# Gated linear attention: scores times values for both 64-row chunks in one product, then the products with the states, alternating rows and columns of the array

## The chip, the cores and the metric

The kernel runs on one core of a Trainium2 chip as one program. The metric is device time in microseconds (us). A page of the profile describes one profiled execution; its span runs from the first to the last instruction of the program.

The engines are named as the profile names them: PE is the matmul engine (PEld its weight loads, which run beside the products), DVE the vector engine, ACT the scalar engine, POOL the general engine, SP the engine whose queue issues the loads from memory.

## The reference

A small network of two layers over 256 positions and 1024 channels, in fp32. Each layer is: half a gated feed-forward block (2816 wide), a mixer, half a second feed-forward block. The mixer of layer 0 has retention in one half of its width and gated linear attention (GLA) in the other; layer 1 has a gated recurrence and an mLSTM. The change touches GLA alone: four heads, key width 64, value width 128, chunks of 64 rows. For one head and chunk:

```
b = cumsum(log_a)                       # over the 64 rows
s = (q * exp(b - b_mid)) @ (k * exp(b_mid - b)).T ;  s = tril(s)
intra  = s @ v                          # 64 x 64 times 64 x 128
upd    = (k * exp(b_end - b)).T @ v     # 64 x 128
state' = exp(b_end) * state + upd       # from chunk to chunk
inter  = (q * exp(b)) @ state
out    = intra + inter
```

## The kernel before

The 256 positions are two tiles of 128 rows, t = 0 and t = 1, so each tile holds two GLA chunks (c = 0, 1). All large products (feed-forward, projections in and out of the mixers) are written by `mm3` (L192 to L200) and by `prod` (L513 to L522): weights and activations are split into a high part and a rest (L114, L115, on ACT and DVE), and a product is three matmuls over 512 columns, with all 128 rows and columns of the array. The even mixer projects in units of 512 columns or less (L993 to L1000). A unit's weights are loaded by SP into one of three raw buffers, split into one of five high/rest buffers, and used by tile 0 and, some 1.5 units later, by tile 1 (`LAG`, L30); a buffer is split into again once tile 1 has used it.

The small work of the mixers is written as generators (`gla_chain`, L766 to L873). They are advanced by `tick` (L159): every `mm3` counts its columns, and a step of a chain is put between the large products when its count has run down (`STEPS`, L46). So GLA's small products stand in PE's queue between the products of a projection. The framework lays out each engine's instruction order with a model of its own; `after(x)` (L385) asks that an instruction come behind x on its engine, without a semaphore.

The four heads are laid out in pairs: head hd = 2p + hh. Keys and queries of head hd lie in partitions hh·64 to hh·64+63 of block p, so a product that contracts over them uses the upper (hh = 0) or lower (hh = 1) 64 rows of PE's array. The output rows of chunk c are partitions c·64 to c·64+63 in PSUM, so a product that makes 64 of them uses the left (c = 0) or right (c = 1) 64 columns of the array. "Layout" below is the pair rows*columns that the profile gives for a product, as 64*64. Every fp32 product is two passes of weight load and matmul, and counts twice in the profile.

In `gla_chain`: the scores of both heads hh of a pair are made with 64 rows and 128 columns (L824) and copied through a mask into `gS{hh}` (L825), a 128 x 128 block for each p with chunk 0 and chunk 1 on its diagonal and zeros elsewhere. The states' updates are products of layout 64*64 (L837); the states `Sst[c]` are formed on DVE (L843, L846). In tile 0 there is no state for c = 0. Then, for each hh, p and c in turn, the output of 64 rows is made: scores times values, contracting over all 128 rows but with the 64 columns of the chunk (L866, layout 128*64), and at once, where there is a state, query times state (L869, layout 64*64). One PSUM tile for each hh takes the outputs and is copied to `og` (L870) before the next hh begins. `og` is normalised (L871, L872), gated (L969) and transposed (L988) later.

PSUM is two rings of four tiles, `ps` for the large products and `acc` for the small ones and for accumulations across units.

Of the kernel before, what the change touches and what calls it, by code (L numbers as in the profile page):

```python
# [19 lines left out]
P = 128  # L20
# [33 lines left out]
def f2(ap):  # L54
    return ap.rearrange("p a b -> p (a b)")
# [7 lines left out]
def hybrid_kernel(ctx: ExitStack, tc: tile.TileContext, I, out):  # L63
    nc = tc.nc
    V, S, T, G = nc.vector, nc.scalar, nc.tensor, nc.gpsimd
# [11 lines left out]
    def nm(s):  # L77
        cnt[0] += 1
        return f"{s}_{cnt[0]}"

    def ps_tile(shape=(P, 512), tag="ps"):
        return psum.tile(list(shape), F32, tag=tag, name=nm(tag))

    def mt(tag, shape, bufs=1, dt=F32):
        return pools[-1].tile(list(shape), dt, tag=tag, bufs=bufs, name=nm(tag))
# [293 lines left out]
    C = {}  # L379
# [5 lines left out]
    def after(ins):  # L385

        return tc.issue_after(ins.ins) if ins is not None else nullcontext()
# [322 lines left out]
    def logsigmoid(dst, z, pre, w, bufs=1):  # L710

        e = mt(pre + "e", [P, w], bufs)
        V.scalar_tensor_tensor(out=e, in0=z, scalar=-1.0, in1=z, op0=ALU.mult, op1=ALU.max)
        S.activation(e, e, AF.Exp, scale=-1.0)
        S.activation(e, e, AF.Ln, bias=one, scale=1.0)
        V.scalar_tensor_tensor(out=dst, in0=z, scalar=0.0, in1=e, op0=ALU.min, op1=ALU.subtract)

    def head_rms_scale(psO, name):

        sq = mt("sq", [P, 4, P], 1)  # L720
        S.activation(f2(sq), f2(psO), AF.Square)
        ss = mt("hss", [P, 4], 2)
        V.tensor_reduce(out=ss, in_=sq, axis=AX.X, op=ALU.add)
        return rsqrt_mean(ss, P, 4, name)

    def bc4(ap):
        return ap.unsqueeze(2).to_broadcast([P, 4, P])
# [8 lines left out]
    def even_units(w_in, w_lr_up, b_lr, w_out, nxt):  # L736
# [4 lines left out]
        def has(t, *keys):  # L741
            return lambda: all(k in st[t] for k in keys)
# [15 lines left out]
        def body_gq(t, ps, rs):  # L758
            gl = mt("gl", [P, 16])
            S.activation(gl, ps[:, 256:], AF.Copy, scale=rs)  # L760
            chain(gla_chain(t, gl))
            q = mt("gq", [P, 256])
            S.activation(q, ps[:, :256], AF.Copy, scale=rs)
            st[t]["q"] = q

        def gla_chain(t, gl):  # L766
            d = st[t]
            yield STEPS[0]
            pt = ps_tile(tag="acc")
            T.transpose(pt[:16, :P], gl, ident)  # L770
            glT = mt("glT", [16, P])
            V.tensor_copy(glT, pt[:16, :P])
            yield STEPS[1]
            pz = ps_tile(tag="acc")
            T.matmul(pz[:, :256], glT, C["lrup"], start=True, stop=True)
            la = mt("gz", [P, 256])
            V.tensor_tensor(out=la, in0=pz[:, :256], in1=C["blr"], op=ALU.add)
            logsigmoid(la, la, "g", 256)
            yield STEPS[2]

            pb = ps_tile(tag="acc")
            pe = ps_tile(tag="acc")
            T.matmul(pb[:, :256], C["cum"][:, 0:P], la, start=True, stop=True)
            T.matmul(pb[:, 256:], C["cum"][:, P:2 * P], la, start=True, stop=True)
            T.matmul(pe[:, :256], C["cum"][:, 2 * P:3 * P], la, start=True, stop=True)
            for p in range(2):
                T.matmul(pe[:, 256 + 2 * p:258 + 2 * p], la[:, p * P:(p + 1) * P], C["cum"][:, 3 * P:3 * P + 2],
                         start=True, stop=True)
            E1 = mt("E1", [P, 256])
            E2 = mt("E2", [P, 256])  # L790
            E3 = mt("E3", [P, 256], 2)
            E4 = mt("E4", [P, 256])
            dec = mt("dec", [P, 4], 2)
            S.activation(E1, pb[:, 256:], AF.Exp)
            S.activation(E2, pb[:, 256:], AF.Exp, scale=-1.0)
            S.activation(E4, pb[:, :256], AF.Exp)
            S.activation(E3, pe[:, :256], AF.Exp)
            S.activation(dec, pe[:, 256:260], AF.Exp)
            yield has(t, "q", "k")

            q, k = d["q"], d["k"]
            V.tensor_tensor(out=E1, in0=q, in1=E1, op=ALU.mult)
            V.scalar_tensor_tensor(out=E2, in0=k, scalar=0.125, in1=E2, op0=ALU.mult, op1=ALU.mult)
            V.tensor_tensor(out=E4, in0=q, in1=E4, op=ALU.mult)
            V.scalar_tensor_tensor(out=E3, in0=k, scalar=0.125, in1=E3, op0=ALU.mult, op1=ALU.mult)
            yield STEPS[3]
            p1 = ps_tile(tag="acc")
            p2 = ps_tile(tag="acc")
            for p in range(2):
                sl = slice(p * P, (p + 1) * P)  # L810
                T.transpose(p1[:, sl], E1[:, sl], ident)
                T.transpose(p1[:, 256 + p * P:256 + (p + 1) * P], E2[:, sl], ident)
                T.transpose(p2[:, sl], E4[:, sl], ident)
            qkT = mt("gqkT", [P, 4, P])
            V.tensor_copy(f2(qkT), p1)
            qiT = mt("gqiT", [P, 2, P], 2)
            S.copy(f2(qiT), p2[:, :256])
            yield STEPS[4]

            for hh in range(2):  # L820
                psS = ps_tile(tag="acc")
                r = slice(hh * 64, hh * 64 + 64)
                for p in range(2):
                    T.matmul(psS[:, p * P:(p + 1) * P], qkT[r, 2 + p, :], qkT[r, p, :], start=True, stop=True)  # L824
                V.copy_predicated(f2(C[f"gS{hh}"]), C["gmask"], psS[:, :256])  # L825
            yield has(t, "gv")
            v = d["gv"]
            if t == 1:
                yield lambda: "gstate" in C
            Sst = [C["gstate"] if t == 1 else None, None, None]  # L830
            upd = []
            for c in range(2 if t == 0 else 1):
                pu = ps_tile(tag="acc")
                r = slice(c * 64, c * 64 + 64)
                for hd in range(4):
                    p, hh = hd // 2, hd % 2
                    T.matmul(pu[hh * 64:hh * 64 + 64, p * P:(p + 1) * P], E3[r, hd * 64:hd * 64 + 64],  # L837
                             v[r, hd, :], start=True, stop=True)
                upd.append(pu)
            for c, pu in enumerate(upd):  # L840
                sn = mt("gst", [P, 2, P], 3)
                if Sst[c] is None:
                    V.tensor_copy(f2(sn), pu[:, :256])  # L843
                else:
                    for p in range(2):
                        V.scalar_tensor_tensor(out=sn[:, p, :], in0=Sst[c][:, p, :],  # L846
                                               scalar=dec[:, 2 * p + c:2 * p + c + 1],
                                               in1=pu[:, p * P:(p + 1) * P], op0=ALU.mult, op1=ALU.add)
                Sst[c + 1] = sn
            if t == 0:  # L850
                C["gstate"] = Sst[2]
            yield STEPS[5]
            o = mt("og", [P, 4, P], 2)
            on = o.rearrange("p (a b) c -> p a b c", a=2)
            for hh in range(2):
                po = ps_tile(tag="acc")
                last = None
                r = slice(hh * 64, hh * 64 + 64)
                for p in range(2):
                    hd = 2 * p + hh  # L860
                    sl = slice(p * P, (p + 1) * P)
                    for c in range(2):
                        cc = slice(c * 64, c * 64 + 64)
                        some = Sst[c] is not None
                        with after(last):
                            last = T.matmul(po[cc, sl], C[f"gS{hh}"][:, p, cc], v[:, hd, :], start=True,  # L866
                                            stop=not some)
                            if some:
                                last = T.matmul(po[cc, sl], qiT[r, p, cc], Sst[c][r, p, :], start=False, stop=True)  # L869
                V.tensor_copy(on[:, :, hh, :], po[:, :256].rearrange("p (a b) -> p a b", a=2))  # L870
            r4 = head_rms_scale(o, "r4g")  # L871
            V.tensor_tensor(out=o, in0=o, in1=bc4(r4), op=ALU.mult)  # L872
            d["og"] = o  # L873
# [568 lines left out]
```

## Time and profile before

| | |
|---|---|
| median of 3 runs | 975.63 us (975.37 to 976.59) |
| profiled execution, its own time | 975.24 us |
| its span | 973.5 us |
| mean granted clock of PE | 0.997 |
| PE busy | 954.9 us (98%) |
| DVE busy | 807.7 us (83%) |
| ACT busy | 602.5 us (62%) |
| mean busy share of the 16 DMA engines on the one load queue | 54.4% |

A busy time is a sum of the durations of an engine's instructions; matmuls are pipelined and overlap, so for PE the distance from start to start says more than the durations. A row of the timeline merges neighbours of one kind: start, time from the first start to the last end, engine, line, operation, tile written and read, layout, shape, count, and in brackets the idle time before it with what ended it. Times of rows are us from the start of the span.

### The profile page before, as it was taken

What the parts mean: (1) busy time and instruction counts of PE and PEld (TensorE: products, weight loads), DVE (VectorE), ACT (ScalarE), POOL (GpSimd) and SP (SyncE); (2) the same over time, 40 slices, a digit from 0 to 9 for tenths busy, and PEclk for the clock granted to TensorE, in tenths of its full rate; (3) what the DMA queues carried; (4) which work ended last, traced back from release to release, by engine and by line L of the source; (5) the groups of instructions that cost most, each with busy time, mean ns of one, the idle gap of its engine ahead of it and who ended that gap; (6) DMA issues with size and microseconds to landing.
All of it is one profiled execution on the core that took longest, in us unless ns stands there. A gap on an engine that the chain in (4) does not pass through costs nothing.

```text
span 973.5 us, 11941 instructions
## 1 busy us (share of the span) xinstructions
PE 954.9 (98%) x4576; PEld 787.4 (81%) x4576; DVE 807.7 (83%) x957; ACT 602.5 (62%) x796; POOL 28.3 (3%) x54
## 2 busy tenths in 40 slices
PE   7999999999999999999999999999999999999997
PEld 5877888887788888888788888888888878888885
DVE  5999998577577999897689999885788899989773
ACT  7565666485356665646466656564899767565652
POOL 0000000000000000000010000000000010000000
PEclk9999999999999999999999999999999999999999
DMA  9929444646356837565762649246443692846141
GB/s 300 375 70 338 158 146 153 195 143 209 103 173 200 297 105 284 170 220 178 254 216 66 242 147 318 71 153 189 130 130 131 189 330 71 318 146 244 43 151 44
DMA packets 105025, 180.08 MB, mean 185 GB/s; under 512 B 8052, under 2 KB 55044, under 8 KB 104968
## 3 DMA queue, kind: packets, MB, share of 16 engines
q1 hardware_dynamic: 104968, 179.31, 54.4%
q8 instruction: 36, 0.59, 0.2%
q14 instruction: 21, 0.17, 0.1%
HBM read 178.25 MB, written 1.05 MB: 184 GB/s over the span
## 4 chain that ended last, share of the span: by engine, by line
PE 80%; DVE 10%; ACT 3%; DMA 3%; issue 3%; POOL 1%; SPq 0%; POOLq 0%; ACTq 0%; DVEq 0%
PE ps L519 19%; PE ps L196 10%; PE ps L199 10%; PE ps L197 10%; PE acc L197 8%; PE acc L199 8%; PE acc L196 8%; DVE lo L115 5%; DVE draw L536 1%; DMA raw<-in_ffn_wd_dram 1%; PE ps L546 1%; ACT hi L114 1%; DMA draw<-in_ffn_wgu_dram 1%; PE ps L213 1%; DMA h<-in_x_dram 1%
## 5 line engine op out<-in xcount | busy, mean ns | idle before, releaser
L115 DVE TENSOR_TENSOR lo<-raw,hi 128x512 fp32r<-128x512 f32 (+4 forms) x236 | 276.6, 1201 | 57.3 <-ACT hi L114 56.7
L114 ACT ACTIVATE hi<-raw 128x512 fp32r<-128x512 f32 (+4 forms) x236 | 234.4, 1041 | 54.3 <-PE ps L199 28.1
L196 PE MATMUL ps<-hi,Th 128*128 128x512 f32 (+3 forms) x544 | 213.6, 393 | 1.5 <-ACT Th L227 1.5
L199 PE MATMUL ps<-hi,Tl 128*128 128x512 f32 (+3 forms) x544 | 207.5, 382 | 0.0
L197 PE MATMUL ps<-lo,Th 128*128 128x512 f32 (+3 forms) x544 | 207.5, 382 | 0.0
L115 DVE TENSOR_TENSOR lo<-draw,hi 128x2048 fp32r<-128x2048 f32 x84 | 190.5, 2286 | 9.2 <-ACT hi L114 8.7
L114 ACT ACTIVATE hi<-draw 128x2048 fp32r<-128x2048 f32 x84 | 160.2, 1915 | 37.0 <-DVE draw L536 25.2
L196 PE MATMUL acc<-hi,aT 128*128 128x512 f32 x352 | 138.5, 395 | 0.0
L197 PE MATMUL acc<-lo,aT 128*128 128x512 f32 x352 | 136.9, 390 | 0.9 <-DVE lo L115 0.9
L196 PEld LDWEIGHTS ps<-hi,Th 128*128 128x128 f32 x544 | 103.4, 190 | 20.7 <-ACT Th L227 1.9
L199 PEld LDWEIGHTS ps<-hi,Tl 128*128 128x128 f32 x544 | 103.2, 190 | 19.4
L197 PEld LDWEIGHTS ps<-lo,Th 128*128 128x128 f32 x544 | 103.4, 190 | 17.6 <-DVE lo L115 0.4
L536 DVE TENSOR_TENSOR draw<-draw,draw 128x2048 f32<-128x2048 f32 x48 | 109.6, 2283 | 0.9 <-DMA draw<-in_ffn_wgu_dram 0.9
L199 PE MATMUL acc<-hi,aT 128*128 128x512 f32 x352 | 109.7, 390 | 0.0
L114 ACT ACTIVATE aT<-ps 128x256 fp32r<-128x256 f32 x88 | 32.9, 378 | 86.4 <-PE ps L213 55.1
L197 PEld LDWEIGHTS acc<-lo,aT 128*128 128x128 f32 x352 | 66.1, 188 | 14.3 <-DVE lo L115 1.3
L199 PEld LDWEIGHTS acc<-hi,aT 128*128 128x128 f32 x352 | 66.1, 188 | 14.0
L196 PEld LDWEIGHTS acc<-hi,aT 128*128 128x128 f32 x352 | 66.1, 188 | 13.1
L519 PE MATMUL ps<-lo,Th 128*128 128x512 f32 x144 | 56.3, 391 | 1.3 <-DVE lo L115 1.3
L519 PE MATMUL ps<-hi,Th 128*128 128x512 f32 x144 | 56.9, 395 | 0.1
L519 PE MATMUL ps<-hi,Tl 128*128 128x512 f32 x144 | 56.2, 390 | 0.0
L115 DVE TENSOR_TENSOR aT<-ps,aT 128x256 fp32r<-128x256 f32 x88 | 36.6, 419 | 19.8 <-ACT aT L114 19.4
(343 smaller groups left out, 1203.9 us busy)
## 6 DMA issues: line engine op xcount, KB each, us to landing
draw<-in_ffn_wgu_dram SPq DMA_DIRECT2D x48, 1024.0 KB, 6.6
raw<-in_ffn_wd_dram SPq DMA_DIRECT2D x44, 1024.0 KB, 5.1
raw<-in_ffn_wgu_dram SPq DMA_DIRECT2D x72, 512.0 KB, 5.0
raw<-in_e_w_in_dram SPq DMA_DIRECT2D x13, 1024.0 KB, 5.1
raw<-in_o_w_in_dram SPq DMA_DIRECT2D x9, 1024.0 KB, 5.3
raw<-in_e_w_out_dram SPq DMA_DIRECT2D x4, 1024.0 KB, 5.4
raw<-in_o_w_out_dram SPq DMA_DIRECT2D x4, 1024.0 KB, 4.9
raw<-in_ffn_wgu_dram SPq DMA_DIRECT2D x14, 256.0 KB, 6.3
```

Source lines behind the costliest of these rows:

```text
L114: S.activation(hi2, src2, AF.Copy)
L115: V.tensor_tensor(out=lo2, in0=src2, in1=hi2.bitcast(F32), op=ALU.subtract)
L196: T.matmul(ps, xh[:, k, :], wk[0][:, sl], start=start, stop=False)
L197: T.matmul(ps, xh[:, k, :], wk[1][:, sl], start=False, stop=False)
L199: state["mm"] = T.matmul(ps, xl[:, k, :], wk[0][:, sl], start=False, stop=stop)
L213: T.transpose(pt[:, i * P:(i + 1) * P], src[:, i * P:(i + 1) * P], ident)
L519: state["mm"] = T.matmul(ps, x[a][:, k, :], w[b][:, k, :], start=first and k == 0 and i == 0, stop=k == 3 and i == 2, skip_group_check=not ...
L536: state["dve"] = V.tensor_tensor(out=out, in0=a, in1=b, op=op)
L546: T.transpose(pt[:, i * P:(i + 1) * P], a[:, i * P:(i + 1) * P], ident)
```

## The change

The scores are asked for in an order that alternates hh (the rows of the array) for each p, into two PSUM tiles taken together, and the two masked copies follow both. The output products are reordered and joined: first, for each hh and p, one product of scores times values over all 128 columns, both chunks at once (the off-diagonal blocks of `gS{hh}` are zeros); then, for each p, the products with the states in the order (hh, c) = (0, 0), (1, 1), (0, 1), (1, 0), those without a state left out. Both heads' PSUM tiles are taken at the start, and both copies to `og` follow all products. Only the first product into each PSUM tile starts an accumulation.

```diff
+            psS = [ps_tile(tag="acc") for _ in range(2)]
+            last = None
+            for p in range(2):
+                for hh in range(2):
+                    r = slice(hh * 64, hh * 64 + 64)
+                    with after(last):
+                        last = T.matmul(psS[hh][:, p * P:(p + 1) * P], qkT[r, 2 + p, :], qkT[r, p, :], start=True,
+                                        stop=True)
             for hh in range(2):
-                psS = ps_tile(tag="acc")
-                r = slice(hh * 64, hh * 64 + 64)
-                for p in range(2):
-                    T.matmul(psS[:, p * P:(p + 1) * P], qkT[r, 2 + p, :], qkT[r, p, :], start=True, stop=True)
-                V.copy_predicated(f2(C[f"gS{hh}"]), C["gmask"], psS[:, :256])
+                V.copy_predicated(f2(C[f"gS{hh}"]), C["gmask"], psS[hh][:, :256])
...
+            po = [ps_tile(tag="acc") for _ in range(2)]
+            last = None
+
             for hh in range(2):
-                po = ps_tile(tag="acc")
-                last = None
-                r = slice(hh * 64, hh * 64 + 64)
                 for p in range(2):
-                    hd = 2 * p + hh
-                    sl = slice(p * P, (p + 1) * P)
-                    for c in range(2):
-                        cc = slice(c * 64, c * 64 + 64)
-                        some = Sst[c] is not None
-                        with after(last):
-                            last = T.matmul(po[cc, sl], C[f"gS{hh}"][:, p, cc], v[:, hd, :], start=True,
-                                            stop=not some)
-                            if some:
-                                last = T.matmul(po[cc, sl], qiT[r, p, cc], Sst[c][r, p, :], start=False, stop=True)
-                V.tensor_copy(on[:, :, hh, :], po[:, :256].rearrange("p (a b) -> p a b", a=2))
+                    with after(last):
+                        last = T.matmul(po[hh][:, p * P:(p + 1) * P], C[f"gS{hh}"][:, p, :], v[:, 2 * p + hh, :],
+                                        start=p == 0, stop=False, skip_group_check=True)
+
+            for p in range(2):
+                for hh, c in ((0, 0), (1, 1), (0, 1), (1, 0)):
+                    if Sst[c] is None:
+                        continue
+                    r, cc = slice(hh * 64, hh * 64 + 64), slice(c * 64, c * 64 + 64)
+                    with after(last):
+                        last = T.matmul(po[hh][cc, p * P:(p + 1) * P], qiT[r, p, cc], Sst[c][r, p, :], start=False,
+                                        stop=True, skip_group_check=True)
+            for hh in range(2):
+                V.tensor_copy(on[:, :, hh, :], po[hh][:, :256].rearrange("p (a b) -> p a b", a=2))
```

## Rows read from the trace of the kernel before

**Rows 1.** The page: the busy time of each engine, and the shares of the chain of work that ended last.
```profile
PE 954.9 (98%) x4576; PEld 787.4 (81%) x4576; DVE 807.7 (83%) x957; ACT 602.5 (62%) x796; POOL 28.3 (3%) x54
...
PE 80%; DVE 10%; ACT 3%; DMA 3%; issue 3%; POOL 1%; SPq 0%; POOLq 0%; ACTq 0%; DVEq 0%
```

**Rows 2.** The waits of PE over the whole span: tile and line that waited, what it waited for, us in total, times, longest. The first four of nine, and the last.
```profile
PE ps L264 <- DMA h<-in_x_dram: 5.6, 2, 3.6
PE ps L519 <- DVE lo L115: 1.6, 3, 1.0
PE ps L196 <- ACT Th L227: 1.5, 1, 1.5
PE acc L197 <- DVE lo L115: 0.9, 1, 0.9
...
PE ps L213 <- DVE ffa L447: 0.2, 1, 0.2
```

**Rows 3.** Timeline of PE at the output products of tile 1: the first and last of the sixteen stays, and the large products on either side.
```profile
242.50 0.39 PE L197 MATMUL ps<-lo,Th 128*128 128x512 f32 x1
242.72 0.39 PE L199 MATMUL ps<-hi,Tl 128*128 128x512 f32 x1
243.04 0.43 PE L866 MATMUL acc<-gv,gS 128*64 128x128 f32 x2
243.40 0.43 PE L869 MATMUL acc<-gst,gqiT 64*64 64x128 f32 x2
243.76 0.43 PE L866 MATMUL acc<-gv,gS 128*64 128x128 f32 x2
...
248.46 0.43 PE L869 MATMUL acc<-gst,gqiT 64*64 64x128 f32 x2
248.81 0.50 PE L196 MATMUL ps<-hi,Th 128*128 128x512 f32 x1
```

**Rows 4.** The same for tile 0: the first and last of its eight stays.
```profile
217.02 0.28 PE L197 MATMUL ps<-lo,Th 128*128 128x256 f32 x1
217.14 0.28 PE L199 MATMUL ps<-hi,Tl 128*128 128x256 f32 x1
217.35 0.44 PE L866 MATMUL acc<-gv,gS 128*64 128x128 f32 x4
217.72 0.43 PE L869 MATMUL acc<-gst,gqiT 64*64 64x128 f32 x2
...
219.90 0.43 PE L869 MATMUL acc<-gst,gqiT 64*64 64x128 f32 x2
220.26 0.39 PE L196 MATMUL ps<-hi,Th 128*128 128x256 f32 x1
```

**Rows 5.** Timeline of PE at two sets of four fp32 products of retention with the whole array, L946 and L957, and their neighbours.
```profile
262.84 0.40 PE L199 MATMUL ps<-hi,Tl 128*128 128x512 f32 x1
263.08 1.05 PE L946 MATMUL acc<-rv,rk 128*128 128x128 f32 x8
263.97 1.06 PE L957 MATMUL acc<-rv,rS 128*128 128x128 f32 x8
264.78 0.48 PE L196 MATMUL ps<-hi,Th 128*128 128x512 f32 x1
```

**Rows 6.** Timeline of PE at the states' updates, L837, tile 0.
```profile
214.31 0.68 PE L837 MATMUL acc<-gv,E 64*64 64x128 f32 x16
214.92 0.39 PE L196 MATMUL ps<-hi,Th 128*128 128x256 f32 x1
```

**Rows 7.** The same for tile 1.
```profile
239.63 0.40 PE L197 MATMUL ps<-lo,Th 128*128 128x512 f32 x1
239.86 0.40 PE L199 MATMUL ps<-hi,Tl 128*128 128x512 f32 x1
240.19 0.65 PE L837 MATMUL acc<-gv,E 64*64 64x128 f32 x8
240.77 0.50 PE L196 MATMUL ps<-hi,Th 128*128 128x512 f32 x1
```

**Rows 8.** Timeline at the scores, L824, of tile 1.
```profile
237.94 0.72 PE L824 MATMUL acc<-gqkT 64*128 64x128 f32 x8
238.59 0.19 PEld L196 LDWEIGHTS ps<-hi,Th 128*128 128x128 f32 x1
```

**Rows 9.** Timeline of DVE at what the output products of tile 1 read: the masked copies and the states.
```profile
239.17 0.77 DVE L825 COPY_PREDICATED gS<-gmask,acc 128x256 f32<-128x256 int32 x2
240.89 0.61 DVE L846 SCALAR_TENSOR_TENSOR gst<-gst,dec,acc 128x128 f32<-128x128 f32 x2 [0.95 <-PE acc L837]
```

**Rows 10.** Instructions on `og`: duration min/median/max, first and last start.
```profile
L870 DVE COPY og<-acc x4: 424/424/425, 218.9 to 248.9; 128x256 f32<-128x256 f32 x4
L969 DVE TENSOR_TENSOR og<-og,gate x2: 684/689/694, 289.5 to 306.8; 128x512 f32<-128x512 f32 x2
```

**Rows 11.** Busy time by stretch: the output products of tile 1, and what follows. Columns: stretch, its length, then busy us (and count) of PE, PEld, DVE, ACT, POOL, then the granted clock, the mean busy share of the DMA engines and GB/s.
```profile
242.90:248.80 5.90, 5.90 (x33) 3.03 (x32) 2.02 (x5) 0.00 (x0) 0.00 (x0) 1.00 0.14 53
248.80:275.00 26.20, 26.20 (x134) 21.98 (x134) 18.18 (x36) 14.23 (x27) 2.78 (x4) 1.00 0.32 96
```

**Rows 12.** Timeline of ACT, of DVE and of SP's queue: the first split of weights behind the output products, and the last weight loads issued before them; then, from the page, these loads: count, size, median us from issue to landing.
```profile
251.89 2.20 ACT L114 ACTIVATE hi<-raw 128x512 fp32r<-128x512 f32 x4 [1.88 <-PE ps L199]
...
252.81 2.49 DVE L115 TENSOR_TENSOR lo<-raw,hi 128x512 fp32r<-128x512 f32 x4
...
235.28 4.36 SPq L128 DMA_DIRECT2D raw<-in_e_w_in_dram  x2
...
raw<-in_e_w_in_dram SPq DMA_DIRECT2D x13, 1024.0 KB, 5.1
```

**Rows 13.** Timeline of PE at the unit that reads those weights: its first product, and the first of its fifth channel block.
```profile
254.77 0.48 PE L196 MATMUL ps<-hi,Th 128*128 128x512 f32 x1
...
258.52 0.39 PE L196 MATMUL ps<-hi,Th 128*128 128x512 f32 x1
```

## The prediction

> **What bounds the kernel now.** I read the page first. PE is busy 98% of the span and carries 80% of the chain that ended last [rows 1]; the next engine, DVE, is busy 83% but has 10% of the chain. Then PE's waits: over the whole span it waits for others some 12 us, of which 5.6 are the first input and 1.5 its first split; the longest of the others is 1.0 us [rows 2]. None of the nine names a tile of GLA. So the order of PE's instructions sets the time, and an instruction of PE that goes is time that goes, if nothing else becomes late.
>
> Then PE's timeline at the change. In tile 1 the last large product before the output products starts at 242.72 and the next one at 248.81: 6.09 us [rows 3]. A large product over 512 columns follows its neighbour after 0.22 to 0.24 us, so 5.86 us belong to the output products. They are sixteen stays of two passes each, evenly 0.36 us apart, and from stay to stay the layout changes between 128*64 and 64*64. In tile 0 the stretch is from 217.14 to 220.26, 3.12 us, with a usual step of 0.12 there (256 columns): 3.00 us for eight stays [rows 4].
>
> What does a stay consist of? Eight passes with the whole array follow each other in 0.89 us, so a pass takes 0.11 [rows 5]. Two passes are 0.22; a stay of two takes 0.36. The missing 0.14 is paid for each change of layout. In tile 0 the first kind of stay holds four passes, the left and the right 64 columns of both chunks, and takes 0.37 (217.35 to 217.72) [rows 4]: passes in different columns of the array run beside each other. The states' updates show the same in layout 64*64: eight passes on two quarters of the array take 0.58 us to the next large product [rows 7], sixteen passes on four quarters 0.61 [rows 6]. Four rounds of 0.11 and one change are 0.58; how many quarters work in a round costs nearly nothing.
>
> **The change part by part.**
>
> *Scores times values.* Removed: sixteen passes in tile 1 and sixteen in tile 0 of layout 128*64. Added: in each tile four products with the whole array, eight passes. Those of retention, the same operation, shape and layout, take 0.89 us and join their large neighbours at the usual step [rows 5]. I take 0.89 per tile.
>
> *Products with the states.* Nothing is removed or added in number: eight products in tile 1, four in tile 0. They now stand together, one stay. In tile 1 they are sixteen passes, four on each quarter: four rounds, as in the updates of tile 0, so 0.61 to the next large product [rows 6]. In tile 0 they are eight passes on the two right quarters, rows alternating: four rounds again, 0.58 [rows 7]. Going into the stay costs a change too: before the updates the step is 0.33 (239.86 to 240.19) where 0.23 is usual [rows 7], so 0.10.
>
> *Sum.* Tile 1: 0.89 + 0.10 + 0.61 = 1.60 for 5.86, a gain of 4.26. Tile 0: 0.89 + 0.10 + 0.58 = 1.57 for 3.00, a gain of 1.43. Together 5.69 us.
>
> *Bounds of this term.* If products of different quarters did not overlap in the new order, the stays would be sixteen and eight passes in a row, 16 × 0.11 + 0.14 = 1.90 and 8 × 0.11 + 0.14 = 1.02, and the gain 5.69 − 1.29 − 0.44 = 3.96. If the changes of layout cost nothing at all, the four (0.10 in, 0.14 out, per tile) go: 5.69 + 0.48 = 6.17. I take 5.69, since the updates have the same layout, operands and output size, and cover both counts of passes.
>
> *Scores.* The source asks for both products of one hh, then of the other; the change alternates. But the eight passes of the scores in tile 1 take 0.65 us to the next load of a large product (237.94 to 238.59) [rows 8], less than the 0.89 of eight passes in a row and close to four rounds with a change, 0.58: the two halves of the rows work side by side already. Each half still has four passes to do, so nothing can be gained. Lost would be 0.89 + 0.14 − 0.65 = 0.38 per tile, if alternation undid the overlap; I take 0. The masked copies stand behind both scores before as after, 0.77 us for the two without a pause between them [rows 9].
>
> The Trainium skill speaks otherwise here. "TensorE: Matmul & The Clock Gate", Part 3 (what overlaps and what doesn't), says that weight loads overlap with running matmuls only where the row group differs. By that, two products of one hh in a row would not overlap, and alternation would be worth up to four rounds, 0.44 us, per tile; the sum would be 5.69 + 0.88 = 6.57. The trace of this case disagrees twice: the scores take 0.65, not 0.89 and a change, in the old order, and four passes that differ in columns alone take 0.37 where two take 0.36.
>
> *The two PSUM tiles and the copies.* Both outputs are taken from the `acc` ring of four at once. The tiles held before them, two of scores and one of updates, are free when the copies and state sums have read them: 239.17 + 0.77 = 239.94 and 240.89 + 0.61 = 241.50, against 242.72, when the output products could begin [rows 3, 9]. The new first product needs `gS`, ready at 239.94, and the products with the states need the sum of 241.50: 1.2 us of margin, and 0.99 more while the first eight passes run. All of these move with PE's earlier gain in tile 0, so the margins stay. Nothing new is waited for. The copies of 0.42 us now come both at the end; `og` is next needed by PE's transposes behind L969, at 289.5 for tile 0 and 306.8 for tile 1 [rows 10], some 60 us later: 0.
>
> *What loses its cover.* In the 5.9 us of tile 1, ACT does nothing, DVE 2.0 us and the DMA engines are 14% busy [rows 11]. So no split and hardly a load hides behind the slow products; DVE's 2.0 us are two copies and steps of the rotary products, and in the 26 us behind DVE has 8 us to spare. The next split is what could be late. It waits for PE itself: ACT begins at 251.89, released by a large product [rows 12], so it comes forward with PE. DVE's part begins at 252.81, four pieces in 2.49 us; the unit that reads them starts at 254.77, and their first channel block, the unit's fifth, is read at 258.52 [rows 13]. The first piece is done a quarter of that, 0.62 us, after 252.81, so 5.1 us remain; even DVE's whole 2.0 us moved behind would fit. The loads: the last two are issued at 235.28 and, by that row's end less an issue of 0.36, 239.28, and land 5.1 us later, 244.4 [rows 12]; at the gained 4.26 + 1.43 the split stands at 246.2, still behind them. So I carry the whole gain to the end.
>
> *Against the clock.* The profiled execution took 975.24 us, 0.39 less than the median of the three runs. 975.24 − 5.69 = 969.55; against the median, 975.63 − 5.69 = 969.94. I forecast 969.9.
>
> **The rivals.**
>
> *A. Part of it is lost behind.* The framework lays out each engine's order with a model of its own, and shorter products can move a split or a load by some places far behind. The waits that stand now show the price: 1.0 and 0.9 us each for a rest of weights that comes late [rows 2]. For it: three such waits on L519 exist, so the layout isn't perfect. Against: the order around the change hangs on PE. Two or three new ones, or the serial bound above, give 971.5 to 973.
>
> *B. The alternation of the scores gains.* Were the eight passes of the scores one behind the other today and in four rounds afterwards, 4 × 0.11 us would go in each tile: 975.63 − 5.69 − 0.88 = 969.1. For it: the source asks for one hh behind the other. Against it: eight passes in 0.65 [rows 8], and columns side by side [rows 4].
>
> *C. The change doesn't do what it says.* If the layout of instructions puts large products between the products with the states, each cut adds a way out and in, 0.24 us. Seven cuts in tile 1 and three in tile 0 give 2.4 back: 972.3. For it: chains stand between large products everywhere; against: the stays of before are chained by the same `after` and show not one large product between them [rows 3, 4].
>
> *D. Slower.* One weight load slips behind another in SP's queue, where a new split order frees the raw buffers in another order. A load takes 5.1 us to land [rows 12]; a slip that finds no cover costs that, and two of them 10.2: 975.63 − 5.69 + 10.2 = 980.1. It turns to slower from the point where more than 5.69 us of landing stand bare. Against: the wait for a rest of weights is never over 1.0 us now [rows 2], so some 4 us of cover stand at most places, and the raw buffers are freed in the order of the units, which doesn't change.
>
> **How the numbers follow.** A change of less than 0.2%, 1.95 us, can't be told from none. Forecast (969.0 to 971): 0.78; A 0.09; B 0.03; C 0.06; D 0.04, of which half stays within 0.2%. The range takes in the upper bound of the gain, 6.17 (969.5), and B (969.1), with 0.6 for the spread of the runs, 968.5, and reaches A and C up to 972.8. Faster 0.94, same 0.04, slower 0.02.
>
> **What would show it.** Right: at L866's new place eight passes of layout 128*128 in 0.89 us in both tiles, then one stay of the states in about 0.6 us, and 1.8 us instead of 6.09 from large product to large product in tile 1, 1.7 instead of 3.12 in tile 0; the scores at 0.65 as before; no new name in PE's waits. Wrong: a stay of the states above 1 us; large products between its passes; a wait of PE for L115 or a load that grew by more than 1 us.

## The result, and the profile after

The changed kernel takes 968.58 us (median of four runs, 967.69 to 969.00), the kernel before, timed beside it, 975.50 us (four runs, 974.11 to 976.59). The ratio is 0.9929, with a 95% interval of 0.9913 to 0.9945: 6.9 us less, or between 5.4 and 8.5. Forecast were 969.9 us and 5.69 us less. Two executions of the kernel before in the later sets, of 2476 and 5480 us, stand apart from all others and are in no comparison.

The page of the changed kernel, which answers to [rows 1]: the busy time of each engine, then the shares of the chain that ended last. The profiled execution took 967.69 us, its span 965.9 us.

```profile
PE 946.9 (98%) x4560; PEld 784.1 (81%) x4560; DVE 806.7 (84%) x957; ACT 602.5 (62%) x796; POOL 28.7 (3%) x54
...
PE 87%; DVE 6%; ACT 2%; issue 2%; DMA 1%; POOL 1%; SPq 0%; POOLq 0%; ACTq 0%; DVEq 0%
```

PE has 16 matmuls less: eight products of two passes go in the two tiles together. It is busy 98% as before and carries 87% of the chain that ended last, so it still sets the end.

Timeline of PE at the output products of tile 1, changed kernel; these four rows answer to [rows 3].

```profile
241.03 0.40 PE L199 MATMUL ps<-hi,Tl 128*128 128x512 f32 x1
241.26 1.06 PE L865 MATMUL acc<-gv,gS 128*128 128x128 f32 x8
242.25 0.67 PE L874 MATMUL acc<-gst,gqiT 64*64 64x128 f32 x16
242.85 0.50 PE L196 MATMUL ps<-hi,Th 128*128 128x512 f32 x1
```

The same in tile 0, which answers to [rows 4].

```profile
216.93 0.28 PE L199 MATMUL ps<-hi,Tl 128*128 128x256 f32 x1
217.05 1.05 PE L865 MATMUL acc<-gv,gS 128*128 128x128 f32 x8
218.03 0.66 PE L874 MATMUL acc<-gst,gqiT 64*64 64x128 f32 x8
218.61 0.38 PE L196 MATMUL ps<-hi,Th 128*128 128x256 f32 x1
```

Read the starts, not the durations. In tile 1 sixteen stays have become two, in tile 0 eight. From large product to large product it is 242.85 − 241.03 = 1.82 us where [rows 3] had 6.09, and 218.61 − 216.93 = 1.68 where [rows 4] had 3.12: 4.27 + 1.44 = 5.71 us. The joined products take 0.99 us in tile 1 and 0.98 in tile 0 up to the first pass of the states, and the states' products 0.60 and 0.58 us up to the next large product.

What comes behind: ACT's split of the next weights, DVE's part of it, and the first products of PE's fifth channel block, which read it; these rows answer to [rows 12, 13].

```profile
245.91 2.20 ACT L114 ACTIVATE hi<-raw 128x512 fp32r<-128x512 f32 x4 [1.52 <-PE ps L199]
...
247.20 2.50 DVE L115 TENSOR_TENSOR lo<-raw,hi 128x512 fp32r<-128x512 f32 x4
...
252.54 0.39 PE L196 MATMUL ps<-hi,Th 128*128 128x512 f32 x1
```

ACT still waits for PE, so the split has come forward with PE by 5.98 us (251.89 to 245.91). DVE's first quarter is done 0.62 us after 247.20, and it is read at 252.54: 4.7 us of margin are left of the 5.1.

The rest of the gain shows when the two timelines of PE are laid beside each other, instruction by instruction. In this pair the changed kernel is 0.6 us ahead from the first loads on and 0.2 from 82 us to GLA; 6.0 us ahead at 279 us of its own span; 6.3 at 377; 6.2 at 727; and 7.55 from 743 to the end. So beside GLA's 5.8 there are two places, one of 0.3 us in the second feed-forward block of layer 0 and one of 1.4 us in layer 1. Neither holds an instruction that the change touches.

### The profile page after: what moved, and what is told of

It is laid out like the page before. It is cut to its first block, busy times and chain, and to the rows that moved or that the text cites. A ratio compares the mean times of both kernels' runs of the same rounds, so it can differ in the third digit from the quotient of the medians.

```text
span 965.9 us, 11908 instructions
## 1 busy us (share of the span) xinstructions
PE 946.9 (98%) x4560; PEld 784.1 (81%) x4560; DVE 806.7 (84%) x957; ACT 602.5 (62%) x796; POOL 28.7 (3%) x54
## 4 chain that ended last, share of the span: by engine, by line
PE 87%; DVE 6%; ACT 2%; issue 2%; DMA 1%; POOL 1%; SPq 0%; POOLq 0%; ACTq 0%; DVEq 0%
PE ps L519 21%; PE ps L196 11%; PE ps L199 11%; PE ps L197 11%; PE acc L197 9%; PE acc L199 9%; PE acc L196 9%; DVE lo L115 3%; PE ps L546 1%; PE ps L213 1%; DVE draw L536 1%; DMA draw<-in_ffn_wgu_dram 1%; ACT hi L114 1%; DMA h<-in_x_dram 1%; POOL ms L330 1%
## 5 line engine op out<-in xcount | busy, mean ns | idle before, releaser
L199 PE MATMUL ps<-hi,Tl 128*128 128x512 f32 (+3 forms) x544 | 206.6, 380 | 0.0
L199 PEld LDWEIGHTS ps<-hi,Tl 128*128 128x128 f32 x544 | 102.6, 189 | 19.2
L536 DVE TENSOR_TENSOR draw<-draw,draw 128x2048 f32<-128x2048 f32 x48 | 109.6, 2282 | 0.8 <-DMA draw<-in_ffn_wgu_dram 0.8
L199 PE MATMUL acc<-hi,aT 128*128 128x512 f32 x352 | 109.7, 390 | 0.0
L199 PEld LDWEIGHTS acc<-hi,aT 128*128 128x128 f32 x352 | 66.1, 188 | 14.0
```

The costliest lines, as they stand in the source:

```text
L199: state["mm"] = T.matmul(ps, xl[:, k, :], wk[0][:, sl], start=False, stop=stop)
L536: state["dve"] = V.tensor_tensor(out=out, in0=a, in1=b, op=op)
```

## The experiments

Ten runs were made, in three sets. The kernel before was timed in each set; its medians were 975.35, 976.07 and 975.15 us.

**The two kernels again.** Without an edit, for a second measure of the gain and of what an execution adds by itself. The kernel before:

> The kernel before, once more. Two readings of the difference in the first pair of traces: 5.8 us go in the output products of gated linear attention, and another 1.6 us between 734.8 and 738.5 us of the span of before, where PE's granted clock is 0.56 and eight large products stand 0.43 us apart instead of 0.23. Accident theory: the fall of the clock there is of that execution; this execution shows it elsewhere, shorter or not at all, and a run without it is about 1.6 us shorter. Rival, bound to the kernel: the same eight products run at half clock again, since they follow the same sparse stretch. The time itself: ratio 1.00 either way.

The changed kernel:

> The changed kernel, once more. Theory: the output products take 1.8 us from large product to large product in tile 1 and 1.7 in tile 0, as in its first trace, and the time is 5.7 to 5.9 us below before (ratio 0.994); what its first runs gained beyond that (6.9 us between the medians) is the clock in single executions. Rival: the change also spares the fall of the clock in layer 1 each time; then the gain stays near 7.4 us (ratio 0.9925) and no trace of it has a fall behind 700 us.

Measured: 975.32 us (ratio to the kernel before 0.9999, 0.9991 to 1.0008) and 968.73 us (0.9931, 0.9919 to 0.9943). The stretches of GLA are as in the first pair: 3.12 and 6.09 us in the one, 1.69 and 1.82 in the other.

**The scores alone.** The first part of the change, on the kernel before:

```diff
+            psS = [ps_tile(tag="acc") for _ in range(2)]
+            last = None
+            for p in range(2):
+                for hh in range(2):
...
+                        last = T.matmul(psS[hh][:, p * P:(p + 1) * P], qkT[r, 2 + p, :], qkT[r, p, :], start=True,
+                                        stop=True)
```

> The kernel before with the first part of the change alone: the scores asked for in alternating rows, both masked copies behind. Theory: the halves of the rows overlap in either order; the scores take 0.65 us to the next large product as before, gain 0 us (ratio 1.000). Rival (only neighbours in the order overlap): 0.44 us less per tile, 0.9 us in all (ratio 0.999).

Measured: 975.45 us, ratio 1.0 (0.9992 to 1.0009). PE's timeline at the scores of tile 1 in this kernel:

```profile
237.98 0.39 PE L199 MATMUL ps<-hi,Tl 128*128 128x512 f32 x1
238.29 0.72 PE L826 MATMUL acc<-gqkT 64*128 64x128 f32 x8
238.94 0.50 PE L196 MATMUL ps<-hi,Th 128*128 128x512 f32 x1
```

The eight passes and the way out take 238.94 − 238.29 = 0.65 us, as in [rows 8] to the hundredth. Alternating the rows of the array gives nothing, since both halves were at work already. Rival B falls.

**Grouped, not joined.** The changed kernel, but scores times values in halves by chunk, as before the change, all of them ahead of the states' products:

```diff
-                    with after(last):
-                        last = T.matmul(po[hh][:, p * P:(p + 1) * P], C[f"gS{hh}"][:, p, :], v[:, 2 * p + hh, :],
...
+                    for c in range(2):
+                        cc = slice(c * 64, c * 64 + 64)
+                        with after(last):
+                            last = T.matmul(po[hh][cc, p * P:(p + 1) * P], C[f"gS{hh}"][:, p, cc], v[:, 2 * p + hh, :],
...
```

> The changed kernel, but scores times values are again made for each chunk by itself with 64 columns (twice the products); only the grouping is kept: first all of these, then the products with the states. Theory (rounds and changes of layout count): the two chunks use different columns and run beside each other, so the sixteen passes are eight rounds, 0.89 us, and one more change of layout on the way in, 0.1 to 0.15; tile 1 takes 1.95 us from large product to large product, tile 0 1.8; gain over before 5.4 us, the joining is worth 0.3 us of 5.7. Rival (the halved number of passes is the gain): sixteen passes in a row, 1.78 us, and the gain falls to 3.9 us.

Measured: 969.54 us, ratio 0.9937 (0.9925 to 0.9949). PE's timeline of this kernel in tile 1:

```profile
241.92 0.39 PE L199 MATMUL ps<-hi,Tl 128*128 128x512 f32 x1
242.24 1.09 PE L867 MATMUL acc<-gv,gS 128*64 128x128 f32 x16
243.26 0.67 PE L876 MATMUL acc<-gst,gqiT 64*64 64x128 f32 x16
243.86 0.50 PE L196 MATMUL ps<-hi,Th 128*128 128x512 f32 x1
```

Large to large takes 1.94 us (1.82 in tile 0), only 0.12 and 0.14 more than in the changed kernel. Sixteen passes on half the columns take 1.02 us where eight passes on all of them take 0.99: the left and the right 64 columns work side by side. What joining saves is mainly the change of layout ahead of them: 0.32 us from L199 to the first half, against 0.23 to the first joined product.

**Joined, not grouped.** The changed kernel, but each pair of states' products stands right behind the joined product of its hh and p:

```diff
...
+                    for c in range(2):
+                        if Sst[c] is None:
+                            continue
+                        cc = slice(c * 64, c * 64 + 64)
+                        with after(last):
+                            last = T.matmul(po[hh][cc, sl], qiT[r, p, cc], Sst[c][r, p, :], start=False,
+                                            stop=True, skip_group_check=True)
-            for p in range(2):
-                for hh, c in ((0, 0), (1, 1), (0, 1), (1, 0)):
...
```

> The changed kernel with the joined products of scores times values, but each followed at once by its products with the states, so that the layout changes eight times per tile again. Theory: per (hh, p) two rounds with the whole array (0.22), a change (0.14), two rounds of states (0.22), a change (0.14): 0.72 us, four of them 2.9; from large product to large product 3.1 us in tile 1 (6.09 before) and 3.0 in tile 0 (3.12 before); gain 3.1 us. Rival (the grouping does nothing, the joining does all): as the whole change, 5.7 us.

Measured: 971.45 us, ratio 0.9964 (0.9947 to 0.9981). PE's timeline of this kernel in tile 1, the first two and the last of the four sets:

```profile
242.74 0.40 PE L199 MATMUL ps<-hi,Tl 128*128 128x512 f32 x1
242.98 0.39 PE L867 MATMUL acc<-gv,gS 128*128 128x128 f32 x2
243.29 0.43 PE L874 MATMUL acc<-gst,gqiT 64*64 64x128 f32 x4
243.66 0.49 PE L867 MATMUL acc<-gv,gS 128*128 128x128 f32 x2
244.08 0.44 PE L874 MATMUL acc<-gst,gqiT 64*64 64x128 f32 x4
...
245.65 0.44 PE L874 MATMUL acc<-gst,gqiT 64*64 64x128 f32 x4
246.01 0.50 PE L196 MATMUL ps<-hi,Th 128*128 128x512 f32 x1
```

Large to large takes 3.27 us, and 3.12 in tile 0, just what it took before the change, though eight passes of sixteen are gone there. A set is 0.79 us (243.29 to 244.08): 0.37 for the states' stay and 0.42 for the joined one, two rounds each (a round is the time of one pass, in which passes on other parts of the array can run beside it). Joining without grouping gives 0 + 2.82 us in the trace, grouping without joining 1.30 + 4.15.

With the experiment before, this settles that grouping makes the gain, and not fewer passes. Grouping does two things at once, and no run parts them. It saves changes of layout: from large product to large product there were 17 in tile 1 and 9 in tile 0, and there are 2 in each. And it lets passes work side by side that stood alone between two changes: tile 1 had 16 stays of two rounds, 32, and tile 0 had 16, where each has 12 now (eight joined passes and four rounds of states). At the 0.14 and 0.11 us of the prediction, an estimate from [rows 3, 5], the 22 changes are 3.1 us and the 24 rounds 2.6, together 5.7 of the 5.71 measured. So about half of the gain is changes of layout, the rest rounds.

**The order of the states' products.** The changed kernel, but quarter by quarter instead of alternating rows and columns:

```diff
-            for p in range(2):
-                for hh, c in ((0, 0), (1, 1), (0, 1), (1, 0)):
-                    if Sst[c] is None:
-                        continue
+            for hh, c in ((0, 0), (1, 1), (0, 1), (1, 0)):
+                if Sst[c] is None:
+                    continue
+                for p in range(2):
```

> The changed kernel with the products with the states ordered by quarter of the array: both p of (hh, c) = (0, 0), then both of (1, 1), of (0, 1), of (1, 0). Theory (each quarter works off its own passes, in whatever order the quarters are asked for): four rounds as before, the stay of the states takes 0.58 us in tile 0 and 0.61 in tile 1, time as the changed kernel. Rival (only neighbours in the order overlap, matmuls start strictly in order): four passes on one quarter in a row before the next quarter comes, 10 to 16 rounds in tile 1, 1.3 to 1.9 us, and 6 to 8 in tile 0, 0.9 to 1.0 us; 1.0 to 1.7 us slower than the changed kernel.

Measured: 969.19 us, ratio 0.9939 (0.9922 to 0.9956). PE's timeline of this kernel at the states of tile 1:

```profile
242.50 0.69 PE L874 MATMUL acc<-gst,gqiT 64*64 64x128 f32 x16
243.11 0.50 PE L196 MATMUL ps<-hi,Th 128*128 128x512 f32 x1
```

0.61 us, as with alternation (0.60). Here each quarter gets its four passes in a row, and still all four quarters work at once. So the alternating order that the change writes out is worth nothing; what matters is that the products stand together. The Trainium skill, "TensorE: Matmul & The Clock Gate", Part 3 (what overlaps and what doesn't), says that weight loads overlap with running matmuls only where the row group differs. By that the eight passes on each half of the rows would stand one behind the other, 0.89 us at the pace of the eight passes of [rows 5]; all sixteen take 0.61 here, so the measurement decides against the rule.

**The states' products twice.** Each of them issued two times:

```diff
+                    for _ in range(2):
+                        with after(last):
+                            last = T.matmul(po[hh][cc, p * P:(p + 1) * P], qiT[r, p, cc], Sst[c][r, p, :], start=False,
+                                            stop=True, skip_group_check=True)
...
```

> The changed kernel with every product with a state made twice (the state's part of the output counts double). Theory: four rounds more on the same quarters and no change of layout: the stay grows by 0.43 to 0.45 us in either tile, 0.9 us in all. Rival (a product costs, not a round): eight more products in tile 1 cost twice what four more in tile 0 cost.

PE's timeline of this kernel, at the states of tile 0 and then of tile 1:

```profile
217.72 1.14 PE L875 MATMUL acc<-gst,gqiT 64*64 64x128 f32 x16
218.79 0.39 PE L196 MATMUL ps<-hi,Th 128*128 128x256 f32 x1
...
242.41 1.17 PE L875 MATMUL acc<-gst,gqiT 64*64 64x128 f32 x32
243.51 0.50 PE L196 MATMUL ps<-hi,Th 128*128 128x512 f32 x1
```

The stays grow to 1.07 and 1.10 us, by 0.49 and 0.50, a little more than expected. Tile 0 got eight passes more and tile 1 sixteen, at the same price: the four rounds more, at 0.12 us a round, are what is paid, not the passes. The one execution took 968.19 us; by itself it could not have shown 1.0 us.

This run also speaks to a rival that the prediction does not name: in the old order each product with a state adds to the PSUM block that the product just before it wrote, and the 0.14 us between stays could be a wait for that block, not a change of layout. Here each product adds to the block that its twin just wrote, at 0.12 us a round; and the updates pay 0.10 us on the way in [rows 7], though the large product ahead of them writes another PSUM tile. So the price stands without such a block, though no run changed the layout and left the blocks alone.

**The old length with the new order.** To tell apart whether the 0.3 and 1.4 us outside GLA come from the new order or from everything behind standing 5.7 us earlier, 25 products with the whole array were put ahead of the output products, 6 in tile 0 and 19 in tile 1:

```diff
+            for _ in range((6, 19)[t]):
+                with after(last):
+                    last = T.matmul(po[0][:, :P], C["gS0"][:, 0, :], v[:, 0, :], start=True, stop=True)
```

> The changed kernel with the time put back in the same places: before the joined products, 6 extra products with the whole array in tile 0 and 19 in tile 1 (50 passes of 0.11 us; the products behind overwrite them). Theory (all of the gain is PE's time in these two stretches): 50 x 0.1115 = 5.6 us come back, the time is before less 0.1 us, ratio 1.000; the fall of PE's clock in layer 1 comes or not, by execution. Rival (about 1 us of the measured 6.6 to 6.9 us is something else that the change brings, such as the order on the other engines): the time stays 1 us below before, ratio 0.999.

Measured: 974.54 us, ratio 0.9992 (0.9983 to 1.0001). The interval holds both expectations, so the time decides nothing. The trace says more. The stretches of GLA are 3.03 and 6.06 us, within 0.1 of [rows 3, 4], and the wait in the feed-forward block is there again. It is in DVE's timeline, in the step of `draw` at L536 near 368 us of the kernel before; the brackets give the idle time before an instruction and what ended it. First the kernel before, then this one, then the changed kernel:

```profile
368.74 2.29 DVE L536 TENSOR_TENSOR draw<-draw,draw 128x2048 f32<-128x2048 f32 x1 [0.53 <-DMA draw<-in_ffn_wgu_dram]
```

```profile
367.89 2.29 DVE L536 TENSOR_TENSOR draw<-draw,draw 128x2048 f32<-128x2048 f32 x1 [0.24 <-DMA draw<-in_ffn_wgu_dram]
```

```profile
362.46 2.28 DVE L536 TENSOR_TENSOR draw<-draw,draw 128x2048 f32<-128x2048 f32 x1
```

DVE waits for a load there in all four traces of a kernel with the old order and in this one, 0.24 to 0.53 us, and in no trace of the changed kernel, of the quarter order, of the doubled states or of the joined order; the grouped kernel has it, with 0.39. Where it stands, PE's lag behind the changed kernel's first execution grows by 0.3 to 0.4 us between 279 and 377 us. It isn't simply that loads come earlier the more GLA gains: the grouped kernel gains 5.45 us in GLA and waits, the joined one 2.8 and doesn't.

The DMA view shows one thing that differs. These are its lines for the stretch from the issue of this load on, 361.4 to 365.0 us, in the first execution of the kernel before. The line of q8 gives the packets of an instruction queue, their MB and their share of the DMA engines; the last figure of the other line is the us from issue to landing:

```profile
q8 instruction: 1, 0.02, 1.8%
...
draw<-in_ffn_wgu_dram SPq DMA_DIRECT2D x1, 1024.0 KB, 7.1
```

In the same stretch of the changed kernel, 355.7 to 359.3 us, the line of q8 is not there:

```profile
draw<-in_ffn_wgu_dram SPq DMA_DIRECT2D x1, 1024.0 KB, 5.5
```

A transfer of 16 KB of instructions starts 2.2 to 2.5 us after the issue of the load in five of the six traces with the wait, those of kernels with 4576 matmuls, and the load lands after 6.8 to 7.1 us. In the six traces without it, of kernels with 4560 or 4584 matmuls, that transfer comes before the issue or 5.4 us and more after it, and the load lands after 5.5 to 6.4 us. So the count of PE's instructions may place the transfer, and with it the wait. But the padded kernel, with 4610, waits without it (6.8 us to landing), and no run moved the transfer alone: the cause is not shown.

**The granted clock in layer 1.** The two kernels once more, for the 1.4 us. The kernel before, in the second set:

> The kernel before, a third trace, for the fall of PE's clock in layer 1. Accident theory: not in the same eight products. Rival: again there.

The changed kernel, in the third set:

> The changed kernel, a third trace. Theory: output products 1.69 and 1.82 us; the fall of PE's clock in layer 1, seen in three of four traces with the old order of the output products and in one of six with a new one, is a matter of the execution and can show here too. Rival (the change prevents it): none behind 700 us.

Measured: 974.22 us (one execution) and 968.81 us (ratio 0.9936, 0.9921 to 0.9951). The busy times of one stretch of 3.7 us in layer 1, in four traces; the columns are those of [rows 11], and the granted clock is the third from the end. The kernel before, in the profiled execution of the prediction:

```profile
734.80:738.50 3.70, 3.70 (x11) 2.88 (x10) 3.70 (x8) 2.48 (x4) 0.00 (x0) 0.56 0.79 240
```

The kernel before, third execution:

```profile
734.80:738.50 3.70, 3.70 (x20) 3.07 (x19) 3.70 (x9) 3.67 (x7) 0.00 (x0) 1.00 0.63 190
```

The changed kernel, first execution, the same work 6.4 us earlier:

```profile
728.40:732.10 3.70, 3.70 (x19) 3.08 (x17) 3.70 (x9) 3.67 (x7) 0.00 (x0) 1.00 0.67 217
```

The changed kernel, third execution:

```profile
728.40:732.10 3.70, 3.70 (x12) 2.98 (x11) 3.70 (x8) 2.46 (x4) 0.00 (x0) 0.59 0.76 224
```

Each kernel has it both ways: with the clock at 0.56 to 0.59 PE gets through 11 or 12 large products in the stretch, at 1.00 through some 20. So the fall belongs to the execution, not to the change, and the first pair happened to have it on one side only. Compare like with like: both with the fall, the kernel before in its first and second execution and the changed one in its third, the spans are 973.5, 972.9 and 967.3 us, 6.2 and 5.6 apart; both without it, 972.4 for the kernel before in its third execution and 965.9 and 965.7 for the changed one, 6.5 and 6.7 apart. Some 0.4 us of the latter two are a wait of PE for DVE near 472 us (L546), which no other execution of the kernel before has.

## Why the prediction was right, and where it was short

**What bounds it.** Right. PE's instructions set the time, and those that went are time that went: the gain of the trace at 279 us, 6.0 − 0.2 = 5.8 us, is carried on: at 727 us it is still there, with the 0.3 us of the feed-forward block, to within 0.1 us.

**Scores times values, 0.89 a tile; states, 0.10 in and 0.61 or 0.58.** Right: 0.99 and 0.98 up to the first state's pass, then 0.60 and 0.58. The sum of 5.69 us came out as 5.71. The rows of the updates [rows 6, 7] were the right stand-in for products of the same layout and size that the trace did not yet have in one stay.

**That changes of layout and rounds are paid, not passes.** Right: the grouped kernel has all the passes and 5.45 of the 5.71 us, the joined one has tile 0's passes cut by a third and gains nothing there. How the gain divides between changes and rounds is the estimate above, not a measurement. That the quarters work side by side, so that rounds count and not passes, is shown by the doubled states. The Trainium skill, "TensorEngine Tiling (Array Packing)", section Tiling Modes, says that changing the tiling mode, not just the tile, drains the engine, and gives no price; this trace agrees in that time passes at each change, 0.10 us in and, by a round of 0.11 to 0.12 us, 0.09 to 0.15 us out. What PE does in that time no run here shows. Stays of two passes with the whole array came dearer in the joined kernel, 0.42 us where the prediction's 0.22 and 0.14 give 0.36; that pattern is not in the change.

**Scores, 0.** Right, by the scores alone. The other sum, 6.57 us, had 0.88 us from them that did not come; that the measured gain lies nearer to it than to 5.69 is chance.

**Margins and cover.** Right: the next split kept 4.7 us, and PE's waits hold no new name behind GLA. The one new name, L546 with 0.4 us at 82 us, stands ahead of it, in the first execution of the changed kernel and not in the two others. The copies to `og` (0.75 us for the two, from 242.98) ended no wait of PE.

**The rivals.** A, part lost behind: no, the whole gain is carried on. B: no. C, large products between the states' products: no, the stays are whole in every trace. D, a slipped weight load: no; the one load whose landing matters came earlier, not later.

**Short by 1.3 us**, 968.6 for 969.9: below the 969.0 to 971 that had most of the chance, and just above the 968.5 at which the whole range began. The step that was short is "So I carry the whole gain to the end", with 5.69 us and nothing beside it. Part of the difference is the measurement: 5.7 lies within the interval of the first pair. But all three measured ratios of the changed kernel lie on the same side, and over the 61 runs of the kernel before and 15 of the changed one whose clock is on record the medians are 975.35 and 968.67 us, 6.7 apart, with a 95% interval of 6.1 to 7.2 by resampling those runs. Of this the traces give 5.8 in GLA and 0.3 to 0.4 for the load at L536: the prediction looked for loads that become late, and not for a wait that stands already and could go. The clock is hardly in it: the mean granted clock over these runs is 0.997 for both kernels. The 0.5 us left can't be told from nothing.

## What to carry to other kernels

Count the changes of layout on PE and the rounds, not the passes: putting small products of one layout together saves the changes and lets products on different parts of the array work side by side, and it gave nearly all of this gain; joining them without that gave half of it. Price a stay by rounds on the busiest quarter of the array plus one way in and out, from a neighbour of the same layout in the same trace. Within a stay, the two orders tried here took the same time. When two profiled executions differ by more than the changed stretch, lay their timelines side by side and look at the granted clock where they part, before explaining it by the change.

## What was not expected of the hardware

- Sixteen passes on four quarters of the array, ordered quarter by quarter, take 0.61 us, as in alternating order (0.60): a quarter whose next pass is far back in PE's order did not hold up the others.
- Eight more passes on two quarters and sixteen more on four cost the same, 0.49 and 0.50 us.
- PE's granted clock falls in some executions of either kernel in the middle of the span: behind a stretch of products with four rows (L1122 to L1176 of the kernel before), large products start 0.43 us apart instead of 0.23, as at 1.2 instead of 2.4 GHz. Six of the twelve traces have it, of kernels with the old order and with the new. In the first pair it made 1.4 of the 7.6 us between the two spans.

The timeline of PE there, first profiled execution of the kernel before:

```profile
732.22 1.13 PE L1127 MATMUL acc<-mx,sel 4*128 4x128 f32 x8
733.19 1.05 PE L1176 MATMUL acc<-wi,sel 4*128 4x128 f32 x8
...
736.37 0.63 PE L199 MATMUL ps<-hi,Tl 128*128 128x512 f32 x1
736.79 0.63 PE L196 MATMUL ps<-hi,Th 128*128 128x512 f32 x1
```

Products of the same stretch of the changed kernel, without the fall:

```profile
729.16 0.40 PE L197 MATMUL ps<-lo,Th 128*128 128x512 f32 x1
729.40 0.39 PE L199 MATMUL ps<-hi,Tl 128*128 128x512 f32 x1
```
